# Layer 1's prologue on the counting clock, opened background slots at the attention's start, and a norm's root read from PSUM

## The chip, the cores and the metric

One core of a Trainium2 chip runs the whole kernel. The metric is the device time in microseconds, as the median of three runs. The engines are TensorE (PE, matrix products, with its weight loads), VectorE (DVE), ScalarE (ACT), GpSimd (POOL) and SyncE (SP, which issues the DMAs). Each engine executes its own instruction list in order. Semaphores between the lists make an engine wait.

## The reference, cut to what matters

A two-layer diffusion transformer on 1024 latent tokens (16 rows of 64) and 256 context tokens, width 1024, all in fp32. Layer 0 attends in neighbourhoods, layer 1 is a grouped attention with normalised queries and keys:

```python
def qknorm_gqa_mixer(h_lat, h_ctx, w_qkv, q_gain, k_gain, w_o, ang_row, ang_col, with_ctx_out):
    q, k, v = project_qkv(h_lat, w_qkv, GQA_HEADS, GQA_KV_HEADS)      # 16 and 4 heads of 64
    qc, kc, vc = project_qkv(h_ctx, w_qkv, GQA_HEADS, GQA_KV_HEADS)
    q = axial_rope(rms_norm(q, q_gain), ang_row, ang_col)
    k = axial_rope(rms_norm(k, k_gain), ang_row, ang_col)
    ...
    k_all = jnp.concatenate([kc, k], axis=1)                          # 1280 keys
    v_all = jnp.concatenate([vc, v], axis=1)
        s = jnp.einsum('bqhgd,bshd->bhgqs', q_b, k_all).astype(jnp.float32) * scale
        p = jax.nn.softmax(s, axis=-1).astype(v_all.dtype)
        return jnp.einsum('bhgqs,bshd->bqhgd', p, v_all)
    ...
    y_lat = o @ w_o
```

Around each mixer and each feed-forward network (FFN) stand an RMS norm with a shift and scale from the conditioning vector, and a gated residual. A last RMS norm of the latent tokens, times a gain, is the output.

## The kernel before, in words

**Layout and products.** Activations stand with channels on the partitions: a tile is 128 channels by 512 tokens, and a layer's 1024 channels are eight such tiles for each of two token blocks (block 0 and block 1; the 256 context tokens are a third, narrower block). Every fp32 product is made of three matmuls: operands are split into a high and a low part (`ah`, `al` for activations, `wh`, `wl` for weights), and PE adds ah·wh, al·wh and ah·wl (L781, L782, L783). So one projection of 128 channels to 512 tokens is 24 matmuls. The weights come by DMA as `wr`, ACT casts them to `wh` (L693), and DVE or POOL subtracts to get `wl` (L695).

**Layer 1.** Its prologue (`proj_qk1`, `proj_v`, `finish_qk1`) projects keys and values, normalises them (`T<-sq,hones` on PE, L2181, sums the squares) and rotates them. Then 64 units of attention follow, each one head and 256 queries. In a unit PE makes scores against the context (`X`, L2249, L2250) and the latent keys (`S`, L2265, L2266); DVE takes maxima (L2257), ACT exponentiates into `Pt` (L860), POOL multiplies by the reciprocal row sum (L871), PE transposes (`T<-ident,Pt`, L878), ACT and DVE split the result into high and low `pT` (L886, L891), and PE multiplies by the values (`o<-pT,Vt`, L508). Then ACT copies `o` to `ob` (L900), POOL combines it in three additions with a DMA between (`r`, `z`, L906 to L919), and a DMA stores `z` as a part of `O1d`.

**The background.** While the attention runs, PE also works through a queue of projections: first the rest of layer 1's queries, then the output projection by `w_o` for block 0. `out_split(b)` loads each finished 128-channel tile of `O1d` as `o32` (for which two units must be done), casts it to `ah` on ACT (L2289) and subtracts to `al` on DVE (L2291). `out_part(m)` makes the 24 matmuls for output tile m into a PSUM bank named `ps1`, of which there is one. `out_add` on DVE (L2306) reads that bank, adds the residual and frees it. Block 1's output projection is part of the following FFN stage; its products go to banks `pf`.

**What sets the order.** Nothing is scheduled at run time. A Python program, `Lanes` (`bg`), writes the instruction lists with a model of time. `pump(x)` adds x credits and emits the next projections' matmul triples while credit is left; a triple costs one credit. Work of the other engines in the background is a set of generators that ask for a slot of an engine ("A" ACT, "D" DVE, "G" POOL, "M" PE's sum of squares, "L" the logarithm on ACT). There are two clocks. `tick()` advances 650 ns, gives each engine one slot and pumps one credit. `turn()` advances 227 ns, gives a slot to each engine that the model holds to be free, and pumps a third of a credit. During attention neither runs: `Plan` sorts a table, `ORDER1`, that says at which nanosecond, relative to a unit's start, each step of the unit is written, with a period of 8172 ns between units. The table also has entries for the background (the names in `FILL`): `PF0`, `PF1` pump `r1` credits each (1.262), `AF0` to `AF2`, `DF0`, `DF1`, `GF0`, `GF1` open a slot of ACT, DVE or POOL, and `MS` and `LN` are for the norms. A FILL entry at a late time, such as `PF1` at 19170, is first written more than two periods after the table's start, because its unit is unit 0.

**The output.** The last norm's root `rs` is made on ACT (L177, L179) into an SBUF tile. `output` then scales eight tiles of the block: DVE does six as one instruction each (L2535: tile times gain times `rs`), and for two ACT multiplies by the gain (L2529) and POOL by `rs` (L2532). A DMA stores each. Block 0 is the last.

Of the kernel before, what the change touches and what calls it, by code (L numbers as in the profile page):

```python
# [12 lines left out]
ALU = mybir.AluOpType  # L13
# [18 lines left out]

V_NMIX, V_NFFN, V_NFIN, V_B, V_QG, V_KG, V_C = 0, 16, 32, 40, 136, 137, 138
V_N = 154
CFG = dict(lag=3, tv=5.0, tm=5.0, t1=40.0, t2=55.0, ts=43.0, p0=28, lo="GD", n=39, ra=2.3, rc=0.7, rq=1.1, rb=1.05, gap=263, r1=1.262, lh=300, tk='ADAG', tb=1000000000.0, tg=1, lp='GD')
PERIOD1 = 8172
ORDER1 = {
# [35 lines left out]
def _build(tc, nc, I, O, top):  # L73
    v, s, g, t = nc.vector, nc.scalar, nc.gpsimd, nc.tensor
# [24 lines left out]
    def vec(base, k):  # L99
        return vecs[:, base + k:base + k + 1]  # L100
# [166 lines left out]
    def startup():  # L267

        ET = mybir.EngineType
        with ExitStack() as ph:  # L270
# [10 lines left out]
            def start(at, gen):  # L281

                heapq.heappush(todo, (at, next(count), gen))
# [10 lines left out]
            def load_raw(k, src):  # L294
                raws[k] = wraw.tile([P, D], F32, name="wr")
                if k[0] == "v":
                    dma(out=raws[k][:].rearrange("p (u n) -> p u n", u=2), in_=src.rearrange("u p n -> p u n"))
                else:
                    dma(out=raws[k][:], in_=src)

            def loads():
                W = I["wqkv0"]
                for m in range(KC):
                    load_aw(m)
                    yield 2.9
                    if m < 2:
                        load_x(0, m)
                        yield 2.9
                    if m in (2, 4):
                        k = "k" if m == 2 else "q"  # L310
                        load_raw(k, W[8 if m == 2 else 0])
                        start(now + 3.5, split(k, wsp))
                        yield 1.5
                for i in range(2):
                    load_raw(f"v{i}", W[16:18, :, i * 512:i * 512 + 512])
                    start(now + CFG["tv"], split(f"v{i}", w0))
                    yield 1.5
                for i in range(2):
                    load_x(1, i)
                    yield 2.9  # L320
                xs.append(xp.tile([P, KC, 512], F32, name="x0")[:, :, :256])
                load_x(2, 0, 1)
                yield 2.9
                for w in range(2):
                    dma(out=Cd[w], in_=crow[w][:])
                    yield 1.5
                for m in (1, 9):
                    load_raw(f"u{m}", W[m])
                    yield 1.5
                for _ in bias_steps():  # L330
                    yield 0.7

            def split(k, pool):
                hi = pool.tile([P, D], F32R, name="wh")
                lo = pool.tile([P, D], F32R, name="wl")
                ws[k] = hi, lo
                s.copy(hi[:], raws[k][:])
                yield 1.2
                v.tensor_tensor(lo[:], raws[k][:], hi[:].bitcast(F32), ALU.subtract)
# [4 lines left out]
            def c_rows():  # L344
                for w in range(2):
                    for i in range(2):
                        ps = psm.tile([P, 512], F32, name="ps1")
                        dg = tmp.tile([P, 4, P], F32, name="nsq", bufs=2)
                        v.tensor_tensor(dg[:], ident[:].unsqueeze(1).broadcast_to([P, 4, P]),
                                        silc2[:, 4 * i:4 * i + 4, w:w + 1].broadcast_to([P, 4, P]), ALU.mult)  # L350
                        t.matmul(ps[:], lhsT=ones[:], rhs=dg[:].rearrange("p a n -> p (a n)"), start=True, stop=True)
                        yield 0.8
                        s.mul(crow[w][:, i * 512:i * 512 + 512], ps[:], float(D))
                        yield 0.3

            def stat(b):
                n = BLK[b][1]
                acc = []
                for kc in range(KC):
# [10 lines left out]
                    yield 0.55  # L370
                yield CFG["tm"] if b == 1 else 2.0
                ms = psp.tile([P, 512], F32, name="ms")
# [74 lines left out]
            def first_qk(b):  # L447
# [3 lines left out]
                for kc in range(KC):  # L451
                    while (b, kc) not in ready or b == 0 and min(kc + CFG["lag"], KC - 1) not in ready:
                        yield 0.2
# [20 lines left out]

            for at, gen in [(0.0, loads()), (5.0, c_rows()), (10.0, stat(0)), (CFG["t1"], stat(1)), (CFG["t2"], stat(2)), (28.0, projections())] + \
                    [(CFG["ts"], shifts_ctx())] + \
                    [(max(9.5, a), modulation(m)) for m, a in enumerate((7.0, 13.0, 18.0, 22.0, 25.0, 28.5, 31.5, 34.5))]:
# [32 lines left out]
    class Ring:  # L510

        def __init__(self, n):
            self.n, self.k, self.back = n, 0, set()
# [41 lines left out]
    class Lanes:  # L555
# [90 lines left out]
                    it[3] = self.now if "0" in was else self.now + self.cost + 80  # L646
                    return

        def turn(self):

            self.now += 227
            while self.events and self.events[0][0] <= self.now:
                heapq.heappop(self.events)[2]()
            for e in "TMLADG":
                if self.busy.get(e, 0) <= self.now + 226 and not (e == "G" and self.port["D"] > max(self.now, self.busy["G"])):
                    self.step(e)
            self.pump(1 / 3)

        def place(self, kind):

# [65 lines left out]
        def tick(self, cost=1.0):  # L726

            self.now += 650
            for e in "TML" + CFG["tk"]:
                if self.busy.get(e, 0) < self.now + CFG["tg" if e == "G" else "tb"]:  # L730
# [192 lines left out]
    class Plan:  # L923
# [1 line left out]
        FILL = ("PF0", "PF1", "PF2", "AF0", "AF1", "AF2", "AF3", "DF0", "DF1", "DF2", "DF3",  # L925
                "DF4", "GF0", "GF1", "GF2", "MS", "LN")

        def __init__(self, phases):

            self.steps, t0 = [], 0  # L930
            for k, (period, order, pairs, rate, gap) in enumerate(phases):
                extra = 3 if k == len(phases) - 1 else 0
                for name, at in order.items():
                    for j in range(len(pairs) + extra * (name in self.FILL)):
                        self.steps.append((t0 + at + j * period, name, pairs[j] if j < len(pairs) else None, rate))
                t0 += len(pairs) * period + gap
            self.steps.sort(key=lambda x: x[0])
# [93 lines left out]
    class Ffn:  # L1031
# [208 lines left out]
        def more(self):  # L1240

            self.ring.idle += self.again()
            if self.layer == 0:
                self.raws.idle += self.xrs + self.tmp[3:]
                self.S.idle += self.tmp[:3]
                self.outs.idle += self.Tf
                self.raws.leave(self.early.idle, self.prepared)
            else:
                self.raws.idle += self.xrs
                self.S.idle += self.Tf  # L1250
                self.outs.idle += self.tmp
# [539 lines left out]
    with ExitStack() as ph:  # L1791
# [6 lines left out]
        bg = Lanes(pb)  # L1798
# [247 lines left out]
        for i, job in enumerate(bg.main[:2]):  # L2046
# [4 lines left out]
        pairs = [[Pair0(h, ps, i) for h in range(HEADS) for i in range(3 - ps)] for ps in range(2)]  # L2051
        n = CFG["n"]
        plan = Plan([(PERIODA, ORDERA, pairs[0][:n], CFG["ra"], 0), (PERIODA, ORDERA, pairs[0][n:], CFG["rq"], CFG["gap"]),
                     (PERIODB, ORDERB, pairs[1], CFG["rb"], 0)])
# [414 lines left out]
    ffn1 = Ffn(1, Hd[1], H2d, lambda m: modB[1][:, m, 0:1], lambda m, b: modB[1][:, 24 + m, 0:1])  # L2469
# [10 lines left out]
    live["open"] = True  # L2480
    bg.lo, bg.cap = CFG["lp"], 6.0
    pairs = [Pair1(h, b) for blk in range(2) for h in range(HEADS) for b in (4 * blk, 4 * blk + 2)]
    plan = Plan([(PERIOD1, ORDER1, pairs, CFG["r1"], 0)])
    while bg.pending("kv", (0, 0), "norm1"):
        bg.tick()
    h0.close()
    pb = l1.enter_context(tc.tile_pool(name="pg", bufs=2, reuse_waits="tile"))
    head_setup1(0, 0)
# [2 lines left out]
        return any(job.tag == (1, 0) for job in bg.main)  # L2491

    while busy_banks - {("ps1", 0)} or more():
        bg.tick(float(more()))
    bg.enter("o0", out_split(0))
    bg.enter("o1", out_split(1))
    live["att"] = True
# [22 lines left out]
    def output(b, rs):  # L2520

        left = set(range(0, KC, 2))

        def scale(k0, others):
            for kc in range(k0, k0 + 2):
                c = ffn1.C[b][kc]
                if others:
                    yield "A0"
                    s.mul(c, c, vec(V_NFIN, kc))  # L2529
                    yield from bg.sleep(700)  # L2530
                    yield "G"
                    g.tensor_tensor(c, c, rs, ALU.mult)  # L2532
                else:
                    yield "D0"
                    v.scalar_tensor_tensor(c, c, vec(V_NFIN, kc), rs, ALU.mult, ALU.mult)  # L2535
                dma(out=O[b][:, kc, :], in_=c)
            left.discard(k0)

        for k0 in range(0, KC, 2):
            bg.enter("final", scale(k0, k0 == 4 or b == 1), 0.0, 1)  # L2540
        while left:
            yield ""
# [114 lines left out]
```

## Time and profile before

| | us |
|---|---|
| runs of before | 3013.36, 3013.57, 3020.36 (median 3013.57) |
| the profiled execution | 3018.95, of which the span of the profile is 3017.1 |
| layer 1's prologue, as far as the order differs | about 1641 to 1712.5 |
| start of attention, until the two orders have done the same work | 1712.5 to 1751.1 |
| the rest of attention, PE busy 540.32 of 548.7 | 1751.1 to 2299.8 |
| end of attention and block 0's last output projections | 2299.8 to 2317.7 |
| FFN of layer 1 | 2317.7 to 2980 |
| last norm and output | 2980 to 3017 |

The stages are cut by the trace's start times of the matmuls at which the two orders part and meet again. In the profile, "idle before <-releaser" beside an instruction is the time for which its engine had nothing to do, and what ended that. A releaser is an instruction of another engine, or a DMA.

### The profile page before, as it was taken

Reading aid. Unit: us, or ns where it says so; the run is one execution under the profiler, and the core shown is the slowest. Engines: PE = TensorE matmul, PEld = TensorE weight load, DVE = VectorE, ACT = ScalarE, POOL = GpSimd, SP = SyncE. Lnnn points to the kernel's source line nnn. Section 1 sums busy time; section 2 is a strip of 40 time slices with the busy share of each in tenths; the row PEclk is TensorE's granted clock in tenths of the full one; section 3 lists DMA queues with packets and bytes.
Section 4 is the critical chain, followed back from the end, with each engine's and each line's share of the span. In section 5 each row is a group of like instructions: output and inputs, shape, how many; then the busy total and the mean of one; then the engine's idle time right before and its main releaser. Section 6 shows DMA issues by size and latency. Waiting matters only on the chain.

```text
span 3017.1 us, 50132 instructions
## 1 busy us (share of the span) xinstructions
PE 2915.8 (97%) x16460; PEld 2503.3 (83%) x16460; DVE 2300.5 (76%) x4671; ACT 1621.0 (54%) x3739; POOL 1238.8 (41%) x1105
## 2 busy tenths in 40 slices
PE   7999998999999999999999899999999999999998
PEld 5788997888788888888888788888888878888886
DVE  7478778876798875557777588999887887776776
ACT  4345545776742222234456489899887632333444
POOL 4246556776145451121121256666643354223112
PEclk9999999999999999999999999999999999999999
DMA  7777777887545562249656523333323343224962
GB/s 268 217 223 239 227 217 230 239 244 219 187 147 188 194 225 76 93 152 324 211 192 205 164 83 95 112 98 102 107 75 127 133 140 122 102 105 149 324 217 108
DMA packets 309218, 519.03 MB, mean 172 GB/s; under 512 B 46560, under 2 KB 113248, under 8 KB 308320
## 3 DMA queue, kind: packets, MB, share of 16 engines
q1 hardware_dynamic: 308960, 515.84, 52.7%
q8 instruction: 131, 2.15, 0.3%
q14 instruction: 127, 1.04, 0.1%
HBM read 389.61 MB, written 120.18 MB: 169 GB/s over the span
## 4 chain that ended last, share of the span: by engine, by line
PE 77%; DVE 10%; DMA 4%; ACT 3%; POOL 2%; issue 2%; SPq 1%; DVEq 0%; ACTq 0%; POOLq 0%
PE pf L1472 9%; PE pf L1474 9%; PE pf L1473 9%; PE T L878 5%; PE o L508 5%; PE pf L1721 5%; PE pf L1720 5%; PE pf L1722 5%; PE ps L781 3%; PE ps L783 3%; PE ps L782 3%; PE S L2265 2%; PE S L2266 2%; DVE pT L891 1%; PE pf L1494 1%
## 5 line engine op out<-in xcount | busy, mean ns | idle before, releaser
L871 POOL TENSOR_SCALAR Pt<-Pt,rc 128x1280 f32<-128x1280 f32 (+3 forms) x288 | 298.0, 1035 | 390.3 <-ACT pT L886 144.3
L891 DVE TENSOR_TENSOR pT<-T,pT 128x256 fp32r<-128x256 f32 (+2 forms) x672 | 341.9, 535 | 34.3 <-ACT pT L886 33.8
L886 ACT CAST pT<-T 128x256 fp32r<-128x256 f32 (+2 forms) x672 | 304.5, 477 | 111.9 <-PE T L878 107.5
L878 PE MATMUL T<-ident,Pt 128*128 128x128 f32 x1952 | 302.8, 274 | 24.1 <-POOL Pt L871 23.5
L878 PEld LDWEIGHTS T<-ident,Pt 128*128 128x128 f32 x1952 | 234.7, 140 | 80.7 <-POOL Pt L871 36.9
L508 PE MATMUL o<-pT,Vt 128*128 128x256 f32 x1952 | 295.2, 289 | 2.5 <-DVE pT L891 2.5
L781 PE MATMUL ps<-ah,wh 128*128 128x512 f32 (+1 forms) x688 | 261.2, 380 | 8.0 <-ACT ah L442 4.1
L508 PEld LDWEIGHTS o<-pT,Vt 128*128 128x128 f32 x1952 | 253.8, 189 | 9.9 <-DVE pT L891 6.2
L782 PE MATMUL ps<-al,wh 128*128 128x512 f32 (+1 forms) x688 | 251.3, 365 | 3.0 <-POOL al L132 2.3
L860 ACT ACTIVATE Pt<-S,rc 128x512 f32<-128x512 f32 (+2 forms) x384 | 247.1, 654 | 9.6 <-DVE rc L852 6.4
L783 PE MATMUL ps<-ah,wl 128*128 128x512 f32 (+1 forms) x688 | 250.7, 364 | 0.0
L2257 DVE TENSOR_REDUCE nm<-S 128x1 f32<-128x512 f32 x256 | 169.7, 683 | 35.7 <-PE S L2266 34.0
L963 POOL TENSOR_TENSOR c<-c,c 128x512 f32<-128x512 f32 (+1 forms) x63 | 93.5, 1486 | 249.6 <-DVE c L966 80.4
L966 DVE TENSOR_TENSOR c<-c,c 128x512 fp32r<-128x512 f32 (+1 forms) x166 | 131.0, 803 | 46.4 <-ACT c L1448 33.7
L860 ACT ACTIVATE Pt<-X,rc 128x256 f32<-128x256 f32 x256 | 125.0, 488 | 67.9 <-DVE rc L852 55.1
L1448 ACT CAST wh<-c 128x512 fp32r<-128x512 f32 x112 | 68.8, 618 | 166.2 <-PE pf L1473 66.5
L781 PEld LDWEIGHTS ps<-ah,wh 128*128 128x128 f32 x688 | 131.4, 191 | 21.2 <-ACT ah L442 4.2
L783 PEld LDWEIGHTS ps<-ah,wl 128*128 128x128 f32 x688 | 130.9, 190 | 21.2
L1472 PE MATMUL pf<-c,wh 128*128 128x512 f32 x376 | 146.5, 390 | 0.0
L1473 PE MATMUL pf<-c,wh 128*128 128x512 f32 x376 | 146.5, 390 | 0.0
L1474 PE MATMUL pf<-c,wl 128*128 128x512 f32 x376 | 146.3, 389 | 0.0
L906 POOL TENSOR_TENSOR r<-ob 128x256 f32<-128x256 f32 x144 | 123.5, 857 | 54.7 <-ACT ob L900 53.7
(596 smaller groups left out, 9137.4 us busy)
## 6 DMA issues: line engine op xcount, KB each, us to landing
c<-in_fout SPq DMA_DIRECT2D x119, 256.0 KB, 3.9
wr<-in_wqkv SPq DMA_DIRECT2D x53, 512.0 KB, 4.8
wr<-in_adaT SPq DMA_DIRECT2D x96, 256.0 KB, 3.2
c<-in_fin SPq DMA_DIRECT2D x68, 256.0 KB, 3.0
adaw<-in_adaT SPq DMA_DIRECT2D x64, 256.0 KB, 3.9
wr<-in_wo SPq DMA_DIRECT2D x32, 512.0 KB, 4.4
wr<-in_fin SPq DMA_DIRECT2D x58, 256.0 KB, 2.7
K<-Kd SPq DMA_DIRECT2D x64, 224.0 KB, 5.2
```

The lines of the kernel that those rows point to most:

```text
L508: t.matmul(o_ap, lhsT=u.V[:, kb, :], rhs=u.pT[:, i, :], start=i == 0, stop=i == len(u.blocks) - 1)
L781: t.matmul(ps, lhsT=hi[:, c], rhs=ah[:, kc, :n], start=kc == 0, stop=False)
L782: t.matmul(ps, lhsT=hi[:, c], rhs=al[:, kc, :n], start=False, stop=False)
L783: t.matmul(ps, lhsT=lo[:, c], rhs=ah[:, kc, :n], start=False, stop=kc == KC - 1)
L860: s.activation(u.Pt[:, off:off + u.wid[c]], u.S[c], AF.Exp, bias=u.min, scale=u.sign, accum_out=u.rc[:, 3 + c:4 + c])
L871: g.tensor_scalar(Pt, Pt, u.rc[:, 2:3], 1.0, ALU.mult, ALU.mult)
L878: t.transpose(T[:, i * P:(i + 1) * P], u.Pt[:, (i0 + i) * P:(i0 + i + 1) * P], ident[:])
L886: s.copy(u.pT[:, i0:i0 + n, :P], u.T[c])
L891: v.tensor_tensor(u.pT[:, i0:i0 + n, P:], u.T[c], u.pT[:, i0:i0 + n, :P].bitcast(F32), ALU.subtract)
L1472: t.matmul(ps[:], lhsT=r32(hi[:, c]), rhs=bh, start=k == 0, stop=False)
L1473: t.matmul(ps[:], lhsT=r32(hi[:, c]), rhs=bl, start=False, stop=False)
L1474: t.matmul(ps[:], lhsT=r32(lo[:, c]), rhs=bh, start=False, stop=k == 3)
```

## The change

Three edits. First, the two loops of layer 1's prologue call `turn()` in place of `tick()`; `turn` gets an argument that switches its pump off where `tick(0.0)` had done so. Second, `Plan` takes a `ramp` of 2.5: FILL entries that would stand one to six periods before unit 0 are written too, where their time is not before -1400, and a PF entry among these pumps 2.5 credits. `r1` goes from 1.262 to 1.2. Third, for block 0 the output takes a PSUM bank, ACT copies `rs` into it, and DVE's scalings read it from there; one of DVE's six tiles goes to ACT and POOL.

```diff
-CFG = dict(... r1=1.262, ...)
+CFG = dict(... r1=1.2, ...)
-        def turn(self):
+        def turn(self, products=True):
...
-            self.pump(1 / 3)
+            if products:
+                self.pump(1 / 3)
...
-        def __init__(self, phases):
+        def __init__(self, phases, ramp=0.0):
             self.steps, t0 = [], 0
+            period, order, pairs, rate, gap = phases[0]
+            for name in self.FILL if ramp else ():
+                for j in range(-6, 0):
+                    at = order.get(name, -1e9) + j * period
+                    if at >= -1400:
+                        self.steps.append((at, name, None, ramp))
...
-    plan = Plan([(PERIOD1, ORDER1, pairs, CFG["r1"], 0)])
+    plan = Plan([(PERIOD1, ORDER1, pairs, CFG["r1"], 0)], 2.5)
     while bg.pending("kv", (0, 0), "norm1"):
-        bg.tick()
+        bg.turn()
...
     while busy_banks - {("ps1", 0)} or more():
-        bg.tick(float(more()))
+        bg.turn(more())
...
     def output(b, rs):
+        ps = None
+        if b == 0:
+            ps, free = yield from ffn1.bank()
+            yield "A0"
+            s.copy(ps[:], rs)
...
-                if others:
+                if others or b == 0 and kc == 7:
                     yield "A0"
                     s.mul(c, c, vec(V_NFIN, kc))
...
-                    v.scalar_tensor_tensor(c, c, vec(V_NFIN, kc), rs, ALU.mult, ALU.mult)
+                    v.scalar_tensor_tensor(c, c, vec(V_NFIN, kc), rs if ps is None else ps[:], ALU.mult, ALU.mult)
```

The lists of PE have the same matmuls in both kernels. Their order differs in layer 1 only, from the prologue (about 1641 us) to the last unit of attention (about 2310 us); both FFNs have the same order. Line numbers after the change are larger by one from L657 and by eight from about L940, and the numbers behind names differ.

On DVE, at the end of the prologue, before the change. `c42` to `c44` take the values' split (L2137), `wl` is the low part of a weight that PE waits for, `xn` and `pl` belong to the norms of keys and queries:

```order
L2137 TENSOR_TENSOR c43_17819<-S_18204,c43_17819 128x4x64
L2137 TENSOR_TENSOR c42_17820<-S_18234,c42_17820 128x4x64
L2137 TENSOR_TENSOR c44_17818<-S_18265,c44_17818 128x4x64
L695 TENSOR_TENSOR wl_18294<-wr_18034,wh_18293 128x512 x2
L695 TENSOR_TENSOR wl_18320<-wr_18108,wh_18319 128x512 x2
L2189 SCALAR_TENSOR_TENSOR xn_18358<-xn_18358,vecs_69,rs_18380 128x256
L2209 TENSOR_TENSOR pl_18406<-xn_18358,ph_18405 128x256
```

And after it:

```order
L2145 TENSOR_TENSOR c43_17817<-S_18202,c43_17817 128x4x64
L2145 TENSOR_TENSOR c42_17818<-S_18235,c42_17818 128x4x64
L696 TENSOR_TENSOR wl_18292<-wr_18006,wh_18291 128x512
L2145 TENSOR_TENSOR c44_17816<-S_18263,c44_17816 128x4x64
L696 TENSOR_TENSOR wl_18292<-wr_18006,wh_18291 128x512
L696 TENSOR_TENSOR wl_18318<-wr_18106,wh_18317 128x512 x2
L2197 SCALAR_TENSOR_TENSOR xn_18356<-xn_18356,vecs_69,rs_18378 128x256
L2217 TENSOR_TENSOR pl_18393<-xn_18356,ph_18392 128x256
```

The first half of the weight `wl_18292` (before: `wl_18294`) has moved ahead of the last value tile, `c44`; its second half still stands behind it.

On PE, in the first unit of attention, before the change: from the first latent score to the next unit's context scores. `ps1_18472` is the background's projection:

```order
L2265 MATMUL S_18508<-K1_18304,Qs_18312 128x512
L2266 MATMUL S_18508<-K2_18305,Qs_18312 128x512
L2265 MATMUL S_18512<-K1_18304,Qs_18312 128x512
L2266 MATMUL S_18512<-K2_18305,Qs_18312 128x512
L2265 MATMUL S_18523<-K1_18304,Qs_18312 128x512
L2266 MATMUL S_18523<-K2_18305,Qs_18312 128x512
L2265 MATMUL S_18526<-K1_18304,Qs_18312 128x512
L2266 MATMUL S_18526<-K2_18305,Qs_18312 128x512
L781 MATMUL ps1_18472<-ah0_17414,wh_18430 128x512
L782 MATMUL ps1_18472<-al0_17415,wh_18430 128x512
L783 MATMUL ps1_18472<-ah0_17414,wl_18431 128x512
L2249 MATMUL X_18550<-K1_18304,Qs_18312 128x256
```

After it, from the second pair of scores on, up to the norm's sum `T<-sq,hones`, behind which the third and fourth pairs follow:

```order
L2273 MATMUL S_18508<-K1_18302,Qs_18310 128x512
L2274 MATMUL S_18508<-K2_18303,Qs_18310 128x512
L782 MATMUL ps1_18473<-ah0_17414,wh_18429 128x512
L783 MATMUL ps1_18473<-al0_17415,wh_18429 128x512
L784 MATMUL ps1_18473<-ah0_17414,wl_18430 128x512
L782 MATMUL ps1_18473<-ah0_17414,wh_18429 128x512
L783 MATMUL ps1_18473<-al0_17415,wh_18429 128x512
L784 MATMUL ps1_18473<-ah0_17414,wl_18430 128x512
L782 MATMUL ps1_18473<-ah0_17414,wh_18429 128x512
L783 MATMUL ps1_18473<-al0_17415,wh_18429 128x512
L784 MATMUL ps1_18473<-ah0_17414,wl_18430 128x512
L2189 MATMUL T_18531<-sq_18506,hones_10510 128x512
```

Nine matmuls of background projection and one sum of squares now stand between the second and the third pair of scores, where before all four pairs stood back to back.

On PE, at the end of attention, before the change: the last unit's transposes, and its two halves of `o`. `ps1_26634` is an output projection, the last but one of block 0:

```order
L878 MATMUL T_26695<-ident_71,Pt_26632 128x128 x2
L878 MATMUL T_26698<-ident_71,Pt_26632 128x128 x4
L878 MATMUL T_26703<-ident_71,Pt_26632 128x128 x4
L508 MATMUL o_26710<-pT_26659,Vt_25536 128x256 x10
L781 MATMUL ps1_26634<-ah0_21291,wh_26095 128x512
L782 MATMUL ps1_26634<-al0_21292,wh_26095 128x512
L783 MATMUL ps1_26634<-ah0_21291,wl_26096 128x512
L508 MATMUL o_26710<-pT_26708,Vt_25536 128x256 x10
L781 MATMUL ps1_26634<-ah0_21291,wh_26095 128x512
L782 MATMUL ps1_26634<-al0_21292,wh_26095 128x512
L783 MATMUL ps1_26634<-ah0_21291,wl_26096 128x512
```

After it, the last two units; `ps1_26717` is the last output projection but one:

```order
L879 MATMUL T_26633<-ident_71,Pt_26567 128x128 x2
L879 MATMUL T_26637<-ident_71,Pt_26567 128x128 x4
L879 MATMUL T_26647<-ident_71,Pt_26567 128x128 x4
L508 MATMUL o_26604<-pT_26602,Vt_25532 128x256 x10
L879 MATMUL T_26674<-ident_71,Pt_26624 128x128 x2
L879 MATMUL T_26677<-ident_71,Pt_26624 128x128 x4
L879 MATMUL T_26682<-ident_71,Pt_26624 128x128 x4
L508 MATMUL o_26689<-pT_26644,Vt_25532 128x256 x10
L508 MATMUL o_26689<-pT_26687,Vt_25532 128x256 x10
L782 MATMUL ps1_26717<-ah0_21168,wh_26204 128x512
```

No projection stands between the last transposes and products any more. All 48 matmuls of the last two output projections (`ps1_26717`, then `ps1_26778`) follow behind the last `o`, where 30 did before.

On DVE at the same place, before the change. `al1_24786<-o32_26777` is the subtraction of `out_split` for the last tile of attention output, and L2306 is `out_add`, which frees the bank `ps1`:

```order
L891 TENSOR_TENSOR pT_26708<-T_26703,pT_26708 128x4x128
L2306 SCALAR_TENSOR_TENSOR al2_21294<-ps1_26634,modB1_85,xr_26756 128x512
L695 TENSOR_TENSOR wl_26759<-wr_26344,wh_26758 128x512
L2291 TENSOR_TENSOR al1_24786<-o32_26777,ah1_24785 128x512
L695 TENSOR_TENSOR wl_26759<-wr_26344,wh_26758 128x512
L2306 SCALAR_TENSOR_TENSOR al2_21294<-ps1_26779,modB1_85,xr_26810 128x512
L695 TENSOR_TENSOR wl_26813<-wr_26729,wh_26812 128x512 x2
```

And after it:

```order
L892 TENSOR_TENSOR pT_26687<-T_26682,pT_26687 128x4x128
L696 TENSOR_TENSOR wl_26629<-wr_25966,wh_26628 128x512 x2
L2299 TENSOR_TENSOR al1_24669<-o32_26761,ah1_24668 128x512
L2314 SCALAR_TENSOR_TENSOR al2_21171<-ps1_26717,modB1_85,xr_26772 128x512
L696 TENSOR_TENSOR wl_26775<-wr_26390,wh_26774 128x512 x2
L2314 SCALAR_TENSOR_TENSOR al2_21171<-ps1_26778,modB1_85,xr_26809 128x512
```

Before, the last `al1` stood between the `out_add` of `ps1_26634` and that of `ps1_26779`, the last two projections. Now it stands ahead of the `out_add` of both of the last two.

More of the change, by code (lines that the diff above doesn't have):

```diff
@@ L34 @@
 V_N = 154
-CFG = dict(lag=3, tv=5.0, tm=5.0, t1=40.0, t2=55.0, ts=43.0, p0=28, lo="GD", n=39, ra=2.3, rc=0.7, rq=1.1, rb=1.05, gap=263, r1=1.262, lh=300, tk='ADAG', tb=1000000000.0, tg=1, lp='GD')
+CFG = dict(lag=3, tv=5.0, tm=5.0, t1=40.0, t2=55.0, ts=43.0, p0=28, lo="GD", n=39, ra=2.3, rc=0.7, rq=1.1, rb=1.05, gap=263, r1=1.2, lh=300, tk='ADAG', tb=1000000000.0, tg=1, lp='GD')
 PERIOD1 = 8172
```

## The prediction

> **What bounds the kernel now.** I read the page's engine table and chain first, then the stages, then PE's waits in the stages that the change touches. The first lines of the page, engine busy time with its share of the span, and further down the chain that ended last:
>
> ```profile
> PE 2915.8 (97%) x16460; PEld 2503.3 (83%) x16460; DVE 2300.5 (76%) x4671; ACT 1621.0 (54%) x3739; POOL 1238.8 (41%) x1105
> ...
> PE 77%; DVE 10%; DMA 4%; ACT 3%; POOL 2%; issue 2%; SPq 1%; DVEq 0%; ACTq 0%; POOLq 0%
> ```
>
> PE is the bound, and its work is the same in both kernels. So the change can only win or lose idle time of PE, time at a lower clock, and the last stretch where PE has finished. The busy time by stage shows how much idle there is (columns: stretch, its length, then each engine's busy time; the last three are granted clock, DMA share and GB/s):
>
> ```profile
> 1634.00:1712.50 78.50, 74.19 (x450) 64.97 (x451) 38.56 (x69) 33.55 (x72) 14.92 (x14) 1.00 0.45 139
> 1712.50:1751.10 38.60, 31.04 (x159) 24.07 (x158) 27.50 (x56) 24.91 (x64) 15.67 (x11) 0.91 0.34 115
> 1751.10:2299.80 548.70, 540.32 (x3631) 474.27 (x3631) 491.02 (x1134) 483.00 (x1276) 336.09 (x300) 1.00 0.32 96
> 2299.80:2317.70 17.90, 17.06 (x100) 14.65 (x99) 8.66 (x15) 7.73 (x18) 7.61 (x9) 1.00 0.30 98
> ```
>
> PE idles 4.3 us in the prologue, 7.6 us in the first 38.6 us of attention at a clock of 0.91, 8.4 us in the other 549 us, and 0.8 us at attention's end. Even all of it would be 21 us, 0.7% of the time. PE's waits in the first two stages, with sum, times and longest:
>
> ```profile
> PE S L2265 <- ACT xn L2172: 2.9, 1, 2.9
> PE S L783 <- DVE wl L695: 2.3, 2, 1.3
> PE T L2181 <- ACT c L2177: 1.9, 1, 1.9
> PE S L2265 <- ACT Pt L860: 1.8, 1, 1.8
> PE ps L781 <- ACT xn L2172: 1.0, 1, 1.0
> PE T L2181 <- DVE pT L891: 1.0, 1, 1.0
> PE X L2249 <- ACT Pt L860: 0.5, 1, 0.5
> PE T L878 <- POOL Pt L871: 0.5, 1, 0.5
> ```
>
> **Prologue, -1.7.** The weight waits (1.0 and 1.3 us) are the ones that the new clock can touch; the wait of the sum of squares (L2181, 1.9 us) stands behind the same projection as before and stays. For the 1.3 us, DVE had been idle before the value tile and took the weight behind it:
>
> ```profile
> 1690.16 0.42 DVE L2137 TENSOR_TENSOR c<-S,c 128x256 fp32r<-128x256 f32 x1 [2.41 <-ACT c L2136]
> 1690.50 1.89 DVE L695 TENSOR_TENSOR wl<-wr,wh 128x512 fp32r<-128x512 f32 x3
> ```
>
> The first half of `wl` now stands ahead of that tile and fits into the 2.41 us of idle, so I count 1.2 us. At the other place the order shortens the wait, by 0.3 to 0.8; I take 0.5. Some low parts change between DVE and POOL, and one on POOL (about 1.3 us, as its other tensor operations below) instead of DVE (0.6) could add a wait of 0.7. So the range is -2.5 to +0.5. Three sums of squares stand three to six matmuls earlier. The list of waits names none before these three, so I cost the move at nothing; if their inputs were just in time, each would wait for what it gained, 0.7 us at three matmuls.
>
> **Start of attention, -5.8.** The 2.9 us wait is followed by a low clock (last columns as above; then two rows of PE in it):
>
> ```profile
> 1715.00:1720.00 5.00, 1.88 (x6) 0.72 (x4) 4.21 (x6) 1.52 (x3) 1.54 (x1) 0.77 0.66 194
> 1720.00:1725.00 5.00, 3.26 (x7) 2.11 (x7) 3.25 (x9) 2.23 (x7) 0.25 (x1) 0.55 0.48 160
> ...
> 1722.97 0.63 PE L2266 MATMUL S<-K,Qs 128*128 128x512 f32 x1
> 1723.40 0.63 PE L781 MATMUL ps<-ah,wh 128*128 128x512 f32 x1
> ...
> 1725.29 0.38 PE L2249 MATMUL X<-K,Qs 128*128 128x256 f32 x1 [0.51 <-ACT Pt L860]
> ```
>
> Matmuls of 512 columns start 0.43 us apart there, and 0.23 apart at full clock (2317.48 and 2317.71 further below). Nine of them cost some 2.0 us. Idle 7.6 and clock 2.0 make 9.6 us that this stage could give. After the change, nine matmuls and a sum of squares stand between the second and third pair of scores (2.5 us of work), which covers the 1.8 us wait and most of the 2.9, since the norm's copy `xn` stands earlier on ACT. Both orders have done the same 48 background matmuls by the end of the stage, so nothing is borrowed. What comes new: the next unit's `X` needs the exponentials of the first. From the last score's end of issue (1723.40) to `X` (1725.29) that chain took 1.89 us; three matmuls at full clock cover 0.7 of it, so 1.2 us of wait. POOL's 0.5 stays, about 0.6 is left of the `xn` wait, and the 1.0 us before the stage's long run of projections stays or, with its copy further back on ACT, grows to 2.4. That is 3.3 to 4.7 us left of 9.6: a gain of 4.9 to 6.3, of which I take 5.8. The ends are -7.5 (only `X` and POOL wait) and -4 (the clock falls once more, and its 2.0 us are not won).
>
> The Trainium skill (TensorE: Matmul & The Clock Gate, What's actually happening) says that the clock halves after at least one idle window of about 3.4 us of a free-running count. The trace differs: it fell after 2.86 us, and the measurement decides. By the page, a wait of 2.4 us would leave the clock alone and the gain would be at least 4.9.
>
> **Rest of attention, 0.** Here PE is busy 540.32 of 548.70 us. `r1` at 1.2 and the opened slots spread the projections otherwise, by at most 12 matmuls (2.7 us) at any unit, and the same waits remain: up to 2 us either way.
>
> **End of attention, +7.7.** 18 of the projection matmuls move behind the last `o`. That alone costs nothing, but who frees their bank does. The rows of PE, ACT and DVE at this place before, and PE's wait for the norm after it:
>
> ```profile
> 2308.53 1.36 PE L508 MATMUL o<-pT,Vt 128*128 128x256 f32 x10
> 2312.11 0.50 PE L781 MATMUL ps<-ah,wh 128*128 128x512 f32 x1 [0.84 <-DVE al L2306]
> 2317.48 0.39 PE L783 MATMUL ps<-ah,wl 128*128 128x512 f32 x1
> 2317.71 0.39 PE L781 MATMUL pf<-ah,wh 128*128 128x512 f32 x1
> 2328.17 1.98 PE L190 MATMUL pf<-c,ones 128*128 128x512 f32 x4 [0.73 <-DVE c L144]
> ...
> 2318.82 0.62 ACT L2289 CAST ah<-o 128x512 fp32r<-128x512 f32 x1 [6.60 <-DMA o<-O1d]
> ...
> 2319.47 0.69 DVE L2291 TENSOR_TENSOR al<-o,ah 128x512 fp32r<-128x512 f32 x1 [6.80 <-ACT ah L2289]
> 2320.08 0.69 DVE L695 TENSOR_TENSOR wl<-wr,wh 128x512 fp32r<-128x512 f32 x1
> 2320.68 0.75 DVE L2306 SCALAR_TENSOR_TENSOR al<-ps,modB,xr 128x512 f32<-128x512 f32 x1
> ```
>
> The first matmul of the next projection waits for `out_add` (0.84 us in the second row), because there is one bank `ps1`. The last `o` ended at 2309.9; its way over `ob`, three additions and three DMAs to `o32` ended in the cast at 2318.82 and the subtraction at 2319.47. Until now only the last `out_add` was queued on DVE behind that subtraction, and PE had block 1's products to do. Now the `out_add` of the last projection but one stands behind it too. It can begin at 2320.08 on this clock and frees the bank 0.75 later, 10.9 us after the last `o`. PE has 24 matmuls, 5.4 us, until then: it idles 5.5 us. Then the clock will be low; I take the 2.0 us that it cost after 2.86 us of idle (between 1.7 and 5.4, the latter if all 24 matmuls of the last projection run at 0.43). Block 1 starts 10.9 + 5.5 + 2.0 = 18.4 us after the last `o`, where it was 7.8: +10.6. Against that, the last `o` comes earlier: 18 matmuls are 4.1 us, of which I give back 1.9, about half, since the last two units have no projections left between exponentials, POOL's scaling, transposes and products (ends 0 and 4.1). And the norm's 0.73 us wait goes, its input being no longer late against PE. 10.6 - 2.2 - 0.7 = 7.7, with ends 5.5 and 11.
>
> **Tail, -1.0.** Durations as min, median, max, and two rows of the last stretch:
>
> ```profile
> L2535 DVE SCALAR_TENSOR_TENSOR c<-c,vecs,o x6: 739/745/1799, 3007.2 to 3012.6; 128x512 f32<-128x512 f32 x6
> L2532 POOL TENSOR_TENSOR c<-c,o x10: 1263/1296/1741, 2986.2 to 3009.1; 128x512 f32<-128x512 f32 x10
> L1762 DVE SCALAR_TENSOR_TENSOR c<-pf,modB,c x64: 735/744/751, 1385.0 to 3001.9; 128x512 f32<-128x512 f32 x64
> L900 ACT COPY ob<-o x144: 577/586/625, 151.1 to 2310.0; 128x512 f32<-128x512 f32 x144
> ...
> 3007.20 6.12 DVE L2535 SCALAR_TENSOR_TENSOR c<-c,vecs,o 128x512 f32<-128x512 f32 x6 [4.51 <-ACT o L179]
> 3007.86 2.93 POOL L2532 TENSOR_TENSOR c<-c,o 128x512 f32<-128x512 f32 x2 [9.76 <-ACT c L2529]
> ```
>
> DVE ended at 3013.3, its slowest scaling at 1.80 us beside POOL's. L1762 reads one operand from PSUM and never exceeded 0.751 in 64. After: ACT's copy 0.6 us (nearest row L900, the other way), then DVE's five at 0.75 end at 3011.6. POOL starts 0.6 later, at 3008.5, with three of 1.3 us: 3012.3, now the end. So -1.0; -1.5 if the copy is quick, +0.4 if POOL's take 1.74. The DMA behind it is of the same kind.
>
> The Trainium skill (SBUF — State Buffer, Who interferes with whom) says that a DVE instruction with two SBUF inputs contends with a GpSimd read, and one with at most one does not. By it the tail gives the 1.0; if the stretch came from elsewhere, nothing.
>
> **Sum.** -1.7 - 5.8 + 0 + 7.7 - 1.0 = -0.8 us. The profiled execution took 3018.95 us (span 3017.1), 5.4 above the median; a difference carries over, so 3013.6 - 0.8 = 3012.8. A change under 0.3%, 9 us, is hardly told from none here.
>
> **Rivals.** A: the end does not stall, because the last tile comes to `o32` within the 5.4 us of the last projection but one. Against it: the cast came 9.0 us after `o`, behind three DMAs. Then the end costs 1.9 - 0.7 = +1.2 and the time is 3013.6 - 7.3 = 3006.3; with the prologue and the start at their good ends (-10) it is 3003.8. Chance 0.16.
>
> B, slower: the start of attention is bound by the chain through ACT and DVE (maximum, exponential, copy), and the matmuls put in only move the waits to the next unit. For it: ACT and DVE are busy 25 and 28 of 38.6 us there. Against it: the clock loss and the 2.9 us are waits for one copy. Then the start gives 0, and the time is 3013.6 - 1.7 + 7.7 - 1.0 = 3018.6; it is slower than before from a gain at the start below 5.0. Chance 0.13.
>
> C: the stretch of DVE's scalings stays, reading PSUM or not; the tail gives 0, 3013.8. Chance 0.08, and the others as sized.
>
> D: after the stall the clock stays low for the whole last projection, 5.4 us instead of 2.0: 3016.2. Chance 0.08. My forecast keeps 0.55.
>
> The likeliest case by itself spans 3009 to 3017. The range, from A with a good start to B with a small extra loss, is 3004.5 to 3019. Faster than 3004.5 takes A and both good ends: 0.1. Slower than 3022.6 takes B together with the stall's upper end: 0.04.
>
> **What would show it.** In the changed profile PE should wait some 5.5 us for DVE's L2314 before the last output projection, with a low clock behind it, and no clock loss at 1715 to 1725. The first attention stage should be 5 to 6 us shorter; DVE's scalings of the tail all at 0.75 and POOL last. I am wrong if `out_add` comes ahead of the last subtraction's wait, if the tile's way to `o32` is much shorter, or if waits of the first unit appear in the second at the same size.

## The result, and the profile after

The changed kernel is slower by a little: the ratio to before is 1.0014, 95% interval 1.0008 to 1.0021, which is 4.2 us of 3016. The medians of 20 runs each are 3021.01 against 3016.47 us; one run of the changed kernel was slow (9987 us), and all ratios here and below are of fast runs alone. The three runs of before that the prediction stood on were on the low side (median 3013.57), which makes up 2.9 us of the miss. I forecast 3012.8 us, 0.8 below before, with a range from 3004.5 to 3019.0; the time lies above it.

The profiled execution took 3024.19 us, its span is 3022.2. Two executions begin layer 1 at times up to some microseconds apart whatever the kernel, so I cut both traces at the same matmuls: at the last `pf<-c,c` matmul of layer 0's FFN, at the `X` at which both orders have done the same 48 background matmuls, and at the norm's sum (L190) from which the orders are the same again. The three stretches before, then after (length, busy time by engine, clock, DMA share, GB/s):

```profile
1633.59:1751.15 117.56, 105.56 (x611) 89.14 (x610) 66.47 (x127) 58.91 (x136) 30.59 (x25) 0.97 0.41 130
1751.15:2328.17 577.02, 567.08 (x3771) 496.52 (x3769) 507.96 (x1161) 497.88 (x1305) 345.13 (x309) 1.00 0.32 98
2328.17:3017.10 688.93, 673.43 (x2942) 553.24 (x2942) 506.90 (x702) 279.81 (x476) 201.48 (x138) 0.99 0.45 158
```

```profile
1632.74:1745.96 113.22, 105.53 (x611) 89.45 (x610) 62.05 (x127) 59.59 (x134) 30.05 (x22) 0.98 0.45 135
1745.96:2333.72 587.76, 569.45 (x3772) 498.29 (x3771) 509.09 (x1161) 498.87 (x1305) 344.05 (x309) 0.99 0.32 98
2333.72:3022.20 688.48, 673.64 (x2943) 552.93 (x2941) 501.94 (x700) 280.86 (x478) 202.22 (x139) 0.99 0.45 156
```

The prologue and the start of attention won 4.3 us, the rest of attention with its end lost 10.7, the FFN and the output won 0.5: +5.9 us in these two traces. PE's waits in the changed kernel, first from the prologue into attention, then from its end on:

```profile
PE ps L782 <- ACT xn L2180: 3.0, 1, 3.0
PE T L2189 <- ACT c L2185: 1.9, 1, 1.9
PE X L2257 <- ACT Pt L861: 1.2, 1, 1.2
PE S L2273 <- ACT xn L2180: 1.0, 1, 1.0
...
PE S L784 <- DVE wl L696: 0.2, 1, 0.2
```

```profile
PE ps L782 <- DVE al L2314: 6.6, 1, 6.6
PE pf L1480 <- ACT wh L1456: 2.6, 1, 2.6
PE T L879 <- DVE pT L892: 1.0, 1, 1.0
```

The weight waits of the prologue have all but gone, and the new wait of 1.2 us on `X` is there. But the wait for the copy `xn` ahead of the long run of projections is 3.0 us, where it was 1.0, and PE stands still for 6.6 us ahead of the last output projection. The rows at that stall, from ACT, DVE and PE:

```profile
2314.02 0.62 ACT L2297 CAST ah<-o 128x512 fp32r<-128x512 f32 x1 [8.85 <-DMA o<-O1d]
...
2314.67 0.69 DVE L2299 TENSOR_TENSOR al<-o,ah 128x512 fp32r<-128x512 f32 x1 [8.58 <-ACT ah L2297]
2315.28 0.74 DVE L2314 SCALAR_TENSOR_TENSOR al<-ps,modB,xr 128x512 f32<-128x512 f32 x1
...
2301.36 2.63 PE L508 MATMUL o<-pT,Vt 128*128 128x256 f32 x20
2316.08 0.80 PE L782 MATMUL ps<-ah,wh 128*128 128x512 f32 x1 [6.61 <-DVE al L2314]
2324.19 0.39 PE L782 MATMUL pf<-ah,wh 128*128 128x512 f32 x1
```

`out_add` (L2314) starts right behind the subtraction (L2299), which waits for the cast, which waits for the last tile's DMA. It is the stall that the prediction described, 12.1 us after the last `o` (2304.0) instead of 10.9. The last projection takes 8.1 us from 2316.08 to 2324.19 instead of 5.45.

The tail, groups of the scalings on DVE and POOL by duration (min, median, max in ns), POOL's once from 2992 us on and once for the last stretch alone:

```profile
L2549 DVE SCALAR_TENSOR_TENSOR c<-c,vecs,pf x5: 743/743/748, 3013.6 to 3016.2; 128x512 f32<-128x512 f32 x5
L2546 POOL TENSOR_TENSOR c<-c,o x11: 1270/1292/1743, 2992.0 to 3016.7; 128x512 f32<-128x512 f32 x11
L2546 POOL TENSOR_TENSOR c<-c,o x3: 1270/1275/1278, 3014.3 to 3016.7; 128x512 f32<-128x512 f32 x3
```

No scaling on DVE is stretched any more, POOL's last three aren't either, and POOL's run ends last. From the last norm's first sum (L190) to the end of the span the last stretch is 34.1 us, where it was 34.8.

### The profile page after: what moved, and what is told of

It is laid out like the page before. It is cut to its first block, busy times and chain, and to the rows that moved or that the text cites. A ratio compares the mean times of both kernels' runs of the same rounds, so it can differ in the third digit from the quotient of the medians.

```text
span 3022.2 us, 50139 instructions
## 1 busy us (share of the span) xinstructions
PE 2917.2 (97%) x16460; PEld 2504.6 (83%) x16460; DVE 2294.4 (76%) x4671; ACT 1624.2 (54%) x3741; POOL 1239.2 (41%) x1103
## 5 line engine op out<-in xcount | busy, mean ns | idle before, releaser
L783 PEld LDWEIGHTS ps<-al,wh 128*128 128x128 f32 x688 | 132.4, 193 | 16.4 <-POOL al L132 4.3
```

Source lines behind the costliest of these rows:

```text
L783: t.matmul(ps, lhsT=hi[:, c], rhs=al[:, kc, :n], start=False, stop=False)
```

## The experiments

Each was run in five rounds against before on the same chip. The ratio is that of the times with its 95% interval. The other columns are lengths in the profiled execution, cut as above. Two traces of the same order differ by 1 to 2 us in them (577.02 and 578.71 us for the middle stretch of before and of the kernel with the output's edit alone), so a difference under 2 us there says little by itself. The expectations below quote 1383.75 us for before and 9.3 us for the end; these come from cuts that lay 0.24 us (before) and 0.72 us (the subtraction behind `out_add`) ahead of the last `pf<-c,c`, at which the table cuts. Of the experiments, r1 alone has five runs, the others have 11 or 12.

| kernel | ratio | to `X` | to L190 | sum with the rest |
|---|---|---|---|---|
| before | 1 | 117.56 | 577.02 | 1383.51 |
| changed | 1.0014 (1.0008 to 1.0021) | 113.22 | 587.76 | 1389.46 |
| subtraction behind `out_add` | 0.9994 (0.9985 to 1.0003) | 113.15 | 579.50 | 1379.44 |
| one more POOL slot | 1.0010 (1.0001 to 1.0018) | 110.26 | 586.26 | 1384.54 |
| r1 alone | 1.0032 (1.0020 to 1.0045) | 118.28 | 585.81 | 1392.73 |
| r1 put back | 0.9992 (0.9983 to 1.0001) | 114.32 | 580.28 | 1383.10 |
| both mends | 0.9976 (0.9964 to 0.9989) | 108.35 | 580.79 | 1375.93 |
| counting clock alone | 0.9984 (0.9973 to 0.9995) | 113.23 | 578.81 | 1381.27 |
| slots alone | 0.9994 (0.9985 to 1.0003) | 113.43 | 580.71 | 1383.40 |
| output's edit alone | 1.0003 (0.9991 to 1.0016) | 117.85 | 578.71 | 1384.80 |
| both mends, late pump | 0.9980 (0.9969 to 0.9991) | 109.13 | 581.14 | 1377.10 |

**The subtraction behind `out_add`.** PE's order is that of the changed kernel, word for word; on DVE one instruction changes places with the next.

```diff
             s.copy(oh[:, kc, :], o32[:])
+            while b == 1 and kc == KC - 1 and left["adds"] > 1:
+                yield ""
             yield "D"
```

> The changed kernel, except that the last tile's subtraction (al1) is written behind the out_add of the last output projection but one; PE's order is the changed kernel's. Queue theory (the stall of 6.6 us exists because out_add stands on DVE behind that subtraction): the stall and the low clock behind it go (6.6 + 2.7 us), nothing takes their place, since block 1's first product needs that tile only in its last three matmuls; about 9 us below the changed kernel, some 4.5 us below before (ratio 0.9985). Rival (the tile's way through ob, three additions and three DMAs is the bound, whoever stands behind it): PE waits as long for it at block 1's first product, and the time is within 3 us of the changed kernel's, above before.

Measured: 0.9994 against 1.0014, 6 us less, where 9 were expected. The interval reaches from 4.5 us below before to 0.9 above, so that it is faster than before isn't shown. In the trace it is 10.0 us less: 8.3 in the stretch up to L190, the rest mostly in the FFN, where the clock fell in the changed kernel's trace and not in this one (see the last section). DVE's rows there:

```profile
2310.70 0.75 DVE L2318 SCALAR_TENSOR_TENSOR al<-ps,modB,xr 128x512 f32<-128x512 f32 x1 [3.38 <-PE ps L784]
2315.40 0.69 DVE L2301 TENSOR_TENSOR al<-o,ah 128x512 fp32r<-128x512 f32 x1 [3.95 <-ACT ah L2297]
```

`out_add` now waits for PE and starts 4.7 us ahead of the subtraction. PE waits 0.84 us there, and block 1's products start 11.9 us after the last `o` instead of 20.2. Nothing else waits for the tile. So the stall is a matter of the queue, and the rival (the tile itself is the bound) falls.

**One more POOL slot.** The rows of POOL, ACT and PE at the 3.0 us wait of the changed kernel show where it comes from:

```profile
1734.25 1.33 POOL L872 TENSOR_SCALAR Pt<-Pt,rc 128x1280 f32<-128x1280 f32 x1 [4.02 <-DVE rc L853]
1735.55 1.70 POOL L2217 TENSOR_TENSOR pl<-xn,ph 128x512 fp32r<-128x512 f32 x1
...
1737.28 0.59 ACT L2180 COPY xn<-ps 128x512 f32<-128x512 f32 x1 [1.26 <-POOL pl L2217]
...
1737.91 0.80 PE L782 MATMUL ps<-ah,wh 128*128 128x512 f32 x1 [3.03 <-ACT xn L2180]
1738.51 0.63 PE L783 MATMUL ps<-al,wh 128*128 128x512 f32 x1
```

PE needs the bank `ps1`, which the copy `xn` frees. The copy needs its tile, which POOL's low part `pl` of an earlier projection still reads. And `pl` stands on POOL behind the scaling of the next unit's `Pt`, for which POOL had sat idle 4.0 us. The experiment writes one slot more into the table:

```diff
+            self.steps += [(at, "GFx", None, 0) for at in [19000]]
```

> The changed kernel with one more GpSimd slot at 19000 in the table, so that the low part pl stands on GpSimd ahead of the third unit's scaling instead of behind it, and the copy xn that waits for it stands earlier on ACT. Theory (the 3.0 us wait before the long run of projections and the low clock after it come from GpSimd's order): both go, the first attention stage is 5 us shorter, the time is about 5 us below the changed kernel's, near before. Rival (the chain over ACT and DVE bounds the stage): the wait moves to another place of the first three units, and the time changes by less than 1.5 us.

In the trace the start is 4.9 us shorter from the first `X` on (30.6 for 35.5 us), as the theory has it; the table's column has only 3.0, because in this trace the clock fell once in the prologue, at 1670 us. The times (1.0010 for 1.0014) move by 1.2 us with an uncertainty of about 3, which neither shows nor excludes it. The stretch comes back in the next but two.

**r1 alone.** Before, with `r1=1.2` only.

> The kernel before with r1 = 1.2 alone. Queue theory: r1 alone leaves 48 matmuls behind the last o and puts the subtraction ahead of the last two out_adds, so the stall is there without the other edits; block 1 starts 20 us after the last o instead of 7.8, the last o comes up to 4.1 us earlier, and the time is 7 to 9 us above before (ratio 1.0023 to 1.003). Rival (the stall comes from the opened slots): within 2 us of before.

1.0032, 9.7 us above before; 9.2 in the trace. PE waits 6.4 us for the same `out_add`. The whole loss of the changed kernel, and more, is in this one number.

**r1 put back.** The changed kernel with `r1=1.262`.

> The changed kernel with r1 back at 1.262; 24 matmuls stand behind the last o, and the out_add of the projection before stands ahead of the subtraction. Queue theory: no stall at the end, the gains of prologue (3.4), start (1.8) and tail (0.7) show: 4 to 6 us below before, 8 to 10 below the changed kernel. Rival (other edits cost the time): above before still, 3 to 5 us.

0.9992: below the changed kernel, but only 2.4 us below before instead of 4 to 6, and the interval just includes no change. The expectation overlooked that 24 matmuls behind the last `o` leave PE early at block 1's products. In the trace PE waits there for the last tile's cast (1.4 us) and then for the norm (2.3 us). So too few projections left over cost as well; with the queue mended, the 48 of r1 = 1.2 cover the tile's 12 us almost exactly.

**Both mends.** The two edits above on the changed kernel.

> The changed kernel with both mends: the last subtraction behind the out_add of the last projection but one, and the GpSimd slot at 19000. If the two losses are independent, as their traces say (9.3 us at the end, 4.9 us at the start), the part of the trace from layer 1's prologue on is 8 to 9 us shorter than before's (1383.75 us) and the time is 0.25 to 0.35% below before. Rival (the time gained at the start is waited for later, at the chain of the last tile): only the first mend's 3.6 us below before remain.

0.9976, 7.2 us below before (interval 3.3 to 10.9), and 7.6 in the trace, of which some 1.4 are a fall of the clock in the FFN that this trace doesn't have. The trace is a little under the theory's 8 to 9. By the times alone the rival's 3.6 us lie just inside the interval, and the first mend's interval overlaps this one; the trace decides for the theory, since up to the `X` 9.2 us are won and PE never waits for the last tile at the end. Against before the middle stretch is 3.8 us longer: 18 matmuls more stand behind the last `o` (4.1 us), which itself comes no earlier (558.9 us behind the `X`, before 558.7). The start keeps what the POOL slot gave. POOL, then ACT, at the place of the 3.0 us wait:

```profile
1732.96 1.34 POOL L872 TENSOR_SCALAR Pt<-Pt,rc 128x1280 f32<-128x1280 f32 x1
1734.35 1.28 POOL L2218 TENSOR_TENSOR pl<-xn,ph 128x512 fp32r<-128x512 f32 x1
1738.33 1.34 POOL L872 TENSOR_SCALAR Pt<-Pt,rc 128x1280 f32<-128x1280 f32 x1 [2.69 <-ACT pT L887]
...
1736.45 0.62 ACT L2181 COPY xn<-ps 128x512 f32<-128x512 f32 x1
```

`pl` fills the idle time between two scalings, the copy stands before PE needs the bank, and PE's list of waits has no `ps` row at the start any more.

**Counting clock alone.** Before, with `turn()` in the prologue.

> The kernel before with the counting clock in layer 1's prologue alone. Theory: the two weight waits go (1.05 to 0.15, 1.28 to 0), which with smaller ones is the 2.8 us that the changed kernel's prologue gained; attention's start keeps a clock loss. 2 to 3 us below before. Rival (the prologue's gain is taken back in the start of attention, because the clock leaves other work undone there): within 1 us of before.

0.9984, 4.8 us below before. To the `X` it gains 4.3 us, more than expected, although this trace has a wait of 1.6 us at the beginning of layer 1 that is 0.2 us before: not only the weight waits go, but the 2.9 us wait for `xn` falls to 0.7, and with it the low clock.

**Slots alone.** Before, with the `ramp` of 2.5.

> The kernel before with the opened slots alone (tick clock, r1 1.262). Theory: 24 matmuls of projections in the first units cover the 2.9 and 1.8 us waits, but GpSimd's order may cost a wait before the long run of projections: start of attention 0 to 6 us shorter; at the end 24 matmuls stand behind the last o and cover only 5.4 of the 12 us that the last tile needs, which costs 2 to 4 us there. Sum -3 to +3 us. Rival (the slots are worth the whole 9.6 us of idle and clock there): 5 us or more below before.

0.9994, within the expected band. To the `X` it gains 4.1 us by another way: the 2.9 us wait stays, but what follows is covered. At the end it loses as r1 put back does. **The two together gain 4.3 us to the `X`, no more than each alone.** They take the same idle time, and what the second would add is waited for at POOL's `pl`.

**Output's edit alone.**

> The kernel before with the output's edit alone. Theory: DVE's five scalings take 0.75 each, GpSimd's three end last, the last stretch is 0.5 to 1.0 us shorter. Rival (they are stretched by GpSimd all the same, or the copy adds to the path): 0 to 0.6 us longer. Too small for the times, which should be the same as before; the traces' last stretches decide.

1.0003, the same, as expected. The last stretch is 34.1 us, 0.7 shorter than before's, like that of the changed kernel; the sum of the trace is 1.3 longer, which is the spread of traces.

**Late pump.** The units' last waits (0.5, 0.3 and 1.0 us in the changed kernel) come with missing projections; here 6 matmuls were moved there.

```diff
-                    lanes.pump(rate if pair is None ...)
+                    lanes.pump(2.4 if at > 509115 and live.get("att") else rate if pair is None ...)
```

with `r1=1.15`, and both mends.

> Both mends, with the pump at 1.15 credits until unit 62 and 2.4 after it, so that 6 more projection matmuls stand between the last two units' o and transposes, and 48 still follow the last o. Theory (the last units' waits of 0.5, 0.3 and 1.0 us come from the missing projections): the first two go, the last stays, because nothing stands before those transposes; the attention stage is 1 to 2 us shorter than with both mends, 10 us below before in the trace, 0.25 to 0.4% in the times. Rival (what is put there is missing elsewhere in the attention): the same as with both mends, within 0.5 us.

0.9980 against 0.9976, no difference. All three waits went, but the attention up to the last `o` took 559.6 us instead of 558.9: waits for scaled `Pt`, `pT` and exponentials in the middle are 10.9 us in the trace, where both mends alone had 9.8 over a longer stretch. The rival is nearer; under a microsecond the trace can't tell more.

## Why the prediction was wrong, step by step

The mechanisms were nearly all there; the terms of two steps were off, both to the bad side.

- **Prologue, -1.7:** right in kind, -2.6, just past its good end of -2.5 (80.97 to 77.72 us to the first `X`, less 0.68 for three matmuls that stand behind it now). The two weight waits went from 1.05 and 1.28 to 0.15 and nothing.
- **Start of attention, -5.8: this step failed.** It gave -1.8, which is outside its ends of -7.5 and -4. The prediction let the 1.0 us wait ahead of the long run grow to 2.4 at worst, by the place of the copy in ACT's list. It grew to 3.0, by POOL's list, which the prediction did not follow: the copy was late because `pl` was queued behind a scaling. With 3.0 us the clock fell once more, which the prediction had as its bad end (-4). Of the 4.0 us missed, about 1.5 are the longer wait (the sum left it 1.5) and about 1.6 the clock (3.5 us for eight starts, which took 2.0 before, behind the 1.0 us wait); the rest are mostly smaller waits. The copy's own inputs, one queue further back, were what to look up. With the POOL slot, prologue and start together give 7.3 and, with both mends, 9.2 us; 7.5 was forecast.
- **Rest of attention, 0, and the give-back of 1.9 at its end:** the last two units wait 1.7 us more (0.5, 0.3 and 1.0), where before they did not wait, as said. Another 1.6 us were lost in the middle, inside the 2 us allowed: of the 4.1 us that the last `o` should come earlier, 0.7 came. The 1.6 come with `r1`: in the stretch from the `X` to 9 us before the last `o`'s end, PE idles 9.8 to 10.1 us in the five traces with 1.2 (late pump aside), and 8.1 to 8.6 in the five with 1.262.
- **End of attention, +7.7: right in kind, too small.** From the last `o` to block 1 it is 20.2 us, +12.4 where +10.6 was summed. The tile's way took 12.1 us instead of 10.9 and the low clock cost 2.7 instead of 2.0. The 0.73 us of the norm went, as forecast, with 0.2 more. So 12.4 - 0.7 - 0.9 = 10.8.
- **Tail, -1.0:** -0.7. The engines did what was summed: POOL's three took 3.73 us and ended 1.1 us sooner than DVE's six had. But from the last scaling's end to the end of the span it is 4.1 us behind POOL, where it was 3.8 behind DVE; the prediction took the two for the same.

The sum of what the traces show is -2.6 - 1.8 + 10.8 - 0.7, with 0.2 in the FFN: +5.9. Against the forecast of -0.8, the start accounts for 4.0, the end with the attention for 3.1, tail and FFN for 0.5, and the prologue gives 0.9 back. By the times the change is +4.2, 5.0 more than forecast; 2.9 us more of the miss are the base of three low runs. From 3016.47 the same sum would have given 3015.7, and a range moved along with it would have reached 3021.9 and held the time, with the step at the start as wrong as it is.

Rival A (no stall) is refuted by the 6.6 us. Rival B had the right place and nearly the right size: matmuls put into the start moved the wait rather than removing it. But its cause was a place in POOL's queue, not the length of the chain; one slot undid it. The rival gave 3018.6 and was the nearest of all, in part by luck: it had nothing for the start, which gave 1.8, and 7.7 for the end, which cost 10.8. Rival C falls with the five scalings at 0.743 to 0.748 us. In the Trainium skill (SBUF — State Buffer, Who interferes with whom) the rule on one SBUF input agrees with that. Rival D's low clock for the whole last projection, at 5.4 us, did not come: the drop cost 2.7.

## What to carry to other kernels

When a wait is removed on the bottleneck engine, follow the next one back through every queue that feeds it, not just the engine named beside it: here PE waited for ACT, ACT for POOL, and POOL for its own list order. In an in-order queue an instruction that waits for a long DMA chain belongs behind everything that frees a resource for the bottleneck; one exchange on DVE won back 6 us, more than the 4.2 that the whole change had cost. Two edits that each gain 4 us at the same place need not gain 8.

## What was not expected of the hardware

After a short wait of PE the clock falls or doesn't, and the length of the wait doesn't say which. The same wait of 2.60 to 2.63 us ahead of the same matmul, in the FFN, was followed by half speed in eight of the eleven profiled executions and not in three. In four of the eight the first matmul behind the wait was slow at once (0.79 to 0.80 us). In the other four, the changed kernel among them, it took 0.50 us, as at full speed, and the clock fell 1.0 to 1.3 us after it had started. Before, then the changed kernel:

```profile
2417.53 0.79 PE L1472 MATMUL pf<-ah,wh 128*128 128x512 f32 x1 [2.62 <-ACT wh L1448]
```

```profile
2423.00 0.50 PE L1480 MATMUL pf<-ah,wh 128*128 128x512 f32 x1 [2.62 <-ACT wh L1456]
```

What decides is where the wait lies in a fixed grid of time. In each of the eleven traces all stretches of half clock begin a multiple of 3.41 us apart and last 3.4, 6.8 or 10.2 us (but for the last, which reaches the end of the span). The next rows are windows of that grid around this wait: their length, PE's busy time, the granted clock, DMA share and GB/s. First before, then the changed kernel, then the subtraction behind `out_add`:

```profile
2414.00:2417.40 3.40, 0.92 (x5) 1.00 0.23 77
2417.40:2420.80 3.40, 3.27 (x8) 0.51 0.21 77
```

```profile
2420.60:2424.00 3.40, 1.00 (x3) 0.99 0.37 124
2424.00:2427.40 3.40, 3.40 (x9) 0.50 0.30 101
```

```profile
2411.40:2414.80 3.40, 1.86 (x9) 1.00 0.20 72
2414.80:2418.20 3.40, 2.33 (x9) 1.00 0.26 82
2418.20:2421.60 3.40, 3.40 (x17) 1.00 0.59 183
```

In the first two, 2.4 to 2.5 us of the wait fall into one window, and the clock is halved for the whole next window, although PE has work again. In the third the wait is split, 1.6 us in one window and 1.0 in the next, and the clock stays. All eleven go this way: 2.1 to 2.5 us of the wait in one window were followed by half clock, 1.6 and less were not. Between 1.6 and 2.1 this place shows nothing. The 2.86 us wait of the prediction fits: the clock fell 2.0 us into it, at the end of a window with 2.1 us of idle time.

This fits the free-running window of about 3.4 us of the Trainium skill (TensorE: Matmul & The Clock Gate, What's actually happening). That page has the clock fall after at least one idle window; here a window that was idle for 2.1 of its 3.4 us was enough.

Such a fall cost 1.2 to 1.7 us here: among the seven kernels with the output's edit, the stretch from L190 to the end is 686.8 us in the three traces without it and 688.1 to 688.5 in the four with it. It may be a part of the spread of about 10 us between runs of the same kernel; that part was not measured.
